# Latent attention: transposing the probabilities in groups of eight instead of four, and what moves with them

## The chip, the cores and the metric

One NeuronCore of a Trainium2 chip runs the kernel. The metric is the device time of one execution in microseconds. Three runs of the kernel before took 1213.33, 1215.23 and 1217.88 us; their median is 1215.23. A lower time is better. The engines are named as in the profile: PE is the tensor engine (PEld its weight loads), DVE the vector engine, ACT the scalar engine, POOL GpSimd, SP the engine that issues most transfers.

## The reference

The kernel computes one layer of an encoder on 1024 tokens of width 1024, in float32. A normed input goes through one wide projection. Its parts feed two mixers. Mixer A is a latent attention with 8 heads, dense over all 1024 tokens; mixer B is an attention with dilated windows in three groups of 8 heads. Each mixer's output is multiplied by a gate, projected, gated again, and the two are added, projected once more, added to the input, and normed. The part that the change touches is mixer A:

```python
def one_block(q_blk):
    s = jnp.einsum('bqhd,bkhd->bhqk', q_blk, k).astype(jnp.float32)
    p = jax.nn.softmax(s, axis=-1).astype(v.dtype)
    return jnp.einsum('bhqk,bkhd->bqhd', p, v)
```

Queries and keys have 96 numbers a head, values 64.

## The kernel before

**Precision.** A float32 operand is split in a high and a low part, each in the format fp32r that PE multiplies in one go. `mm3` (lines 143 to 147) makes a product of two split operands in three matmuls: high by high, high by low, low by high. In the trace these are L145, L146 and L147.

**Stages.** The input projection, the dilated mixer, the latent attention (797.4 to 1087.5 us of the span) and the output projection follow one another. All of it is issued in the order in which it is written (`manual_schedule`): each engine has one queue and takes its instructions in that order. An instruction that waits holds up all that stands behind it on its engine.

**The latent attention** works through 32 units. A unit is one head and 256 of the queries, that is two blocks of 128 queries, called b = 0 and b = 1. Units come in pairs: an even unit and the odd unit behind it fill the two halves of one PSUM bank with their weighted values. `mla_attention` (from line 1187) calls `mla_tick(k, c)` four times for each unit k, with c = 0 to 3. A tick issues work of three units at once:

- *Transposes.* The probabilities of unit k lie with queries on the partitions, and the value product needs the keys there. `mla_transposes` (L1063) turns one group: four tiles of 128 by 128, two key blocks by two query blocks, into one PSUM bank. The banks for this are a ring of two, `pt`. Four groups c = 0 to 3 make a unit.
- *High and low part.* ACT copies the bank to `pt_h` (L1065), DVE subtracts that from the bank into `pt_l` (L1071, `mla_low`). `pt_h` and `pt_l` are rings of two as well, so a group's copy reuses the buffer of the group before the last, which its value product must have read.
- *Value product.* `mla_values(k, c)` makes four matmuls of 256 columns (L1087 with the high part, L1088 with the low part) and adds them up in the bank `m_av`. Group 0 of an even unit starts that bank anew.
- *Scores of the next unit.* `mla_scores(k + 1, b)` makes six matmuls of 512 columns (L145 to L147 into `left` or `right`), `mla_maxima` takes the row maxima on DVE (L1047), `mla_exponentials` the exponentials on ACT (L1055, with a read-out of their sum).
- *After an odd unit*, `mla_copied` copies one half of the partitions of `m_av` on ACT (L1094) and `mla_sum` adds it to the other on DVE (L1103). These run in tick 0 of the next, even unit.
- *After the last unit of a pair of heads and a half of the queries* (units 5, 7, 13, 15, 21, 23, 27, 31), `mla_spread` transposes the denominators on PE (L1117) into the next bank of the same ring `pt`, and DVE doubles and inverts them (L1119, L1120). Then follow transfers, a product on POOL (`mla_gated`), one on DVE (`mla_weighted`, L1140) and a split on ACT and POOL (`mla_merged`).
- *Feed.* In ticks 2 and 3, `feed` issues some steps of other projections, so that PE has work while ACT and DVE turn the groups over; a step is one `mm3` of 512 columns. Up to unit 7 these belong to the gates of the input projection, behind it to the projections of the mixers' outputs. The number of steps to a tick is `rate`: 2 in most units, 1 in units 11, 12, 16, 17, 21, 22, 26 and 27.

The order of one unit on PE was, with T for four transposes, S for six score matmuls, V for four value matmuls and F for a feed:

```
tick 0: T(k,0)  S(k+1,0)  V(k-1,3)  [denominators]
tick 1: T(k,1)  S(k+1,1)  V(k,0)
tick 2: T(k,2)  F         V(k,1)
tick 3: T(k,3)  F         V(k,2)
```

After a tick, `mla_attention` runs what has fallen due of the dilated mixer's last sums (DVE L1636, POOL L1640) and of the loads of the last weights.

Of the kernel before, what the change touches and what calls it, by code (L numbers as in the profile page):

```python
# [11 lines left out]
F32R = mybir.dt.float32r  # L12
# [49 lines left out]
class Net:  # L62
# [994 lines left out]
    def mla_transposes(self, k, c):  # L1057

        pt = self.get("pt")
        for c2 in range(2):  # L1060
            for b in range(2):
                kc, o = 2 * c + c2, c2 * 256 + b * 128
                self.nc.tensor.transpose(pt[:, o:o + 128], self.P[k, b][:, 128 * kc:128 * kc + 128], self.ident)  # L1063
        h, l = self.get("pt_h", dtype=F32R), self.get("pt_l", dtype=F32R)
        self.nc.scalar.copy(out=h, in_=pt)  # L1065
        self.pt[k, c] = pt, h, l

# [82 lines left out]

    def mla_tick(self, k, c):

        self.mla_transposes(k, c)
        if c == 0:
            self.mla_low(k, c)
            self.mla_scores(k + 1, 0)
            self.mla_values(k - 1, 3)
            self.mla_copied(k - 1)
            self.mla_spread(k)
            self.mla_maxima(k + 1, 0)  # L1160
            self.mla_sum(k - 1)
            h, u = self.units[k - 1] if k else (0, 0)
            if u == 3 and h < 6:
                self.mla_load_v(h + 2)
        elif c == 1:
            self.mla_exponentials(k + 1, 0)
            self.mla_low(k, c)
            self.mla_scores(k + 1, 1)
            self.mla_values(k, 0)
            self.mla_maxima(k + 1, 1)  # L1170
            self.mla_weighted(k - 1)
            h, u = self.units[k]
            if u == 3 and h < 6:
                self.mla_load_qk(h + 2)
        else:
            if c == 2:
                self.mla_exponentials(k + 1, 1)
            self.mla_low(k, c)
            self.feed(self.rate)
            self.mla_values(k, c - 1)  # L1180
            if c == 2:
                for n in {6: (), 7: (), 8: (5,), 9: (7,)}.get(k, (k - 1,)):
                    self.mla_merged(n, self.nc.gpsimd)
            else:
                self.mla_gated(k)
# [714 lines left out]
```

## Time and profile before

| | us |
|---|---|
| median of three runs | 1215.23 |
| lowest and highest run | 1213.33, 1217.88 |
| the profiled execution | 1215.87 |
| its span (first to last instruction) | 1214.1 |
| PE busy | 1197.5 |
| DVE busy | 739.8 |
| ACT busy | 606.1 |
| POOL busy | 557.5 |

A row of the profile's groups names line, engine, operation, tiles and shapes, then the count, the total busy time in us, the mean of one in ns, and the idle time of the engine just before, with what ended it. A row of the timeline begins with the start and the length of an instruction in us from the span's start; rows that end in x4 are four instructions in one, and a bracket gives idle time of the engine and what ended it. The ends of matmuls are modelled, so the distance from one start to the next tells what a matmul costs, not its length. A row of the stretches gives bounds and length in us, the busy time (and count) of PE, PEld, DVE, ACT and POOL, the granted clock of PE as a share of full speed, and the load of the DMA engines. The tiles of the latent attention show as `bank` (the rings `pt`, `m_av` and `pj`), `left` and `right` (scores), `at_r` and `at_f` (placed by hand in SBUF) and `m_nm` (maxima).

### The profile page before, as it was taken

To read this page: it belongs to the slowest core of one execution; us is meant where nothing else is said; L and a number is where in the kernel's file an instruction comes from. 1 tells how busy PE (TensorE), PEld (TensorE's weight loads), DVE (VectorE), ACT (ScalarE), POOL (GpSimd) and SP (SyncE) were. 2 spreads that over 40 slices of the span, in tenths; PEclk is the share of its full clock that TensorE was granted. 3 is DMA by queue.
4 is the path that set the end of the run, shared out by engine and by line. 5 is a ranking of instruction groups with operands and counts; after the bars stand their busy time and mean duration, and the time that the engine had idled before them with its cause. 6 is when DMAs were issued, how large, how long until landed. Compare 5 with 4: busy or idle time off the path is not lost.

```text
span 1214.1 us, 18210 instructions
## 1 busy us (share of the span) xinstructions
PE 1197.5 (99%) x6343; PEld 1030.1 (85%) x6343; DVE 739.8 (61%) x1289; ACT 606.1 (50%) x1259; POOL 557.5 (46%) x473
## 2 busy tenths in 40 slices
PE   9999999999999999999999999999999999999997
PEld 8888878888888888889889899888888888888886
DVE  6775447466666653345666666566757767669442
ACT  6633346343434435356565657454655656654222
POOL 1413027877777777544374624335820111258322
PEclk9999999999999999999999999999999999999999
DMA  8757983597355642397899898937462534235141
GB/s 282 227 192 267 330 311 108 195 281 194 106 139 153 177 122 108 101 289 212 239 258 274 247 263 245 260 107 188 137 171 78 139 105 123 79 121 181 74 154 52
DMA packets 128924, 221.30 MB, mean 182 GB/s; under 512 B 28024, under 2 KB 66496, under 8 KB 123904
## 3 DMA queue, kind: packets, MB, share of 16 engines
q1 hardware_dynamic: 128832, 220.14, 60.5%
q8 instruction: 50, 0.82, 0.3%
q14 instruction: 42, 0.34, 0.1%
HBM read 149.24 MB, written 70.85 MB: 181 GB/s over the span
## 4 chain that ended last, share of the span: by engine, by line
PE 89%; DMA 5%; POOL 2%; DVE 1%; ACT 1%; issue 1%; SPq 0%; POOLq 0%; ACTq 0%; DVEq 0%
PE bank L145 7%; PE bank L146 7%; PE bank L147 7%; PE pj L146 5%; PE pj L147 5%; PE pj L145 5%; PE bank L1063 4%; PE st_d L146 2%; PE st_a L146 2%; PE st_c L146 2%; PE st_c L147 2%; PE st_a L147 2%; PE st_d L147 2%; PE st_d L145 2%; PE st_a L145 2%; PE st_c L145 2%
## 5 line engine op out<-in xcount | busy, mean ns | idle before, releaser
L152 POOL TENSOR_TENSOR w_l<-w_raw,w_h 128x512 fp32r<-128x512 f32 x175 | 230.1, 1327 | 213.2 <-ACT w_h L151 164.5
L151 ACT CAST w_h<-w_raw 128x512 fp32r<-128x512 f32 x188 | 111.7, 620 | 121.7 <-POOL w_raw L684 98.1
L145 PE MATMUL bank<-at_r,w_h 128*128 128x512 f32 x344 | 141.6, 412 | 0.0
L146 PE MATMUL bank<-at_r,w_h 128*128 128x512 f32 x344 | 135.4, 394 | 0.5 <-POOL at_r L152 0.5
L147 PE MATMUL bank<-at_r,w_l 128*128 128x512 f32 x344 | 135.5, 394 | 0.0
L1071 DVE TENSOR_TENSOR at_r<-bank,at_r 128x512 fp32r<-128x512 f32 x128 | 87.9, 687 | 69.0 <-ACT at_r L1065 68.5
L1065 ACT CAST at_r<-bank 128x512 fp32r<-128x512 f32 x128 | 74.9, 585 | 85.4 <-PE bank L1063 84.8
L684 POOL TENSOR_TENSOR w_raw<-w_raw 128x512 f32<-128x512 f32 x64 | 83.2, 1300 | 6.3 <-DVE w_l L152 5.6
L1063 PE MATMUL bank<-consts,at_f 128*128 128x128 f32 x512 | 76.9, 272 | 0.5 <-DVE at_r L1071 0.5
L147 PEld LDWEIGHTS bank<-at_r,w_l 128*128 128x128 f32 x344 | 64.8, 188 | 14.5
L146 PE MATMUL pj<-w_l,at_r 128*128 128x512 f32 x192 | 75.5, 393 | 1.2 <-DVE w_l L152 1.2
L145 PE MATMUL pj<-w_h,at_r 128*128 128x512 f32 x192 | 75.7, 394 | 0.7 <-ACT w_h L151 0.7
L1336 DVE TENSOR_TENSOR at_r<-bank,at_r 128x512 fp32r<-128x512 f32 x64 | 43.9, 685 | 53.0 <-ACT at_r L1332 52.7
L147 PE MATMUL pj<-w_h,at_r 128*128 128x512 f32 x192 | 75.4, 392 | 0.0
L146 PEld LDWEIGHTS bank<-at_r,w_h 128*128 128x128 f32 x344 | 65.2, 189 | 9.7 <-POOL at_r L152 1.0
L145 PEld LDWEIGHTS bank<-at_r,w_h 128*128 128x128 f32 x344 | 65.0, 189 | 8.9
L1088 PE MATMUL bank<-at_r,at_r 128*128 128x256 f32 x256 | 67.2, 284 | 4.2 <-DVE at_r L1071 4.2
L1087 PE MATMUL bank<-at_r,at_r 128*128 128x256 f32 x256 | 67.2, 283 | 0.0
L1317 ACT ACTIVATE at_f<-at_f,at_f 128x256 f32<-128x256 f32 x128 | 64.1, 505 | 1.4 <-DVE at_f L1310 1.4
L1332 ACT CAST at_r<-bank 128x512 fp32r<-128x512 f32 x64 | 37.5, 586 | 54.3 <-PE bank L1324 53.1
L1063 PEld LDWEIGHTS bank<-consts,at_f 128*128 128x128 f32 x512 | 59.3, 140 | 1.3 <-DVE at_r L1071 0.9
L1088 PEld LDWEIGHTS bank<-at_r,at_r 128*128 128x128 f32 x256 | 48.7, 190 | 10.2 <-DVE at_r L1071 5.1
(335 smaller groups left out, 3287.1 us busy)
## 6 DMA issues: line engine op xcount, KB each, us to landing
w_raw<-wt SPq DMA_DIRECT2D x48, 512.0 KB, 4.0
at_r<-s_dq SPq DMA_DIRECT2D x32, 512.0 KB, 8.0
s_dk<-dq_st SPq DMA_DIRECT2D x80, 128.0 KB, 2.3
s_dv<-dv_st SPq DMA_DIRECT2D x16, 512.0 KB, 3.4
s_dq<-dq_st SPq DMA_DIRECT2D x64, 128.0 KB, 2.4
zt<-s_gt SPq DMA_DIRECT2D x32, 256.0 KB, 3.8
w_raw<-wv SPq DMA_DIRECT2D x24, 256.0 KB, 5.7
at_r<-s_dk SPq DMA_DIRECT2D x8, 576.0 KB, 11.8
```

Source lines behind the costliest of these rows:

```text
L145: mm(out, lh, rh, start=start, stop=False, skip_group_check=skip)
L146: mm(out, lh, rl, start=False, stop=False, skip_group_check=skip)
L147: return mm(out, ll, rh, start=False, stop=stop, skip_group_check=skip)
L151: self.nc.scalar.copy(out=h, in_=raw)
L152: sub.tensor_tensor(out=l, in0=raw, in1=h.bitcast(F32), op=ALU.subtract)
L684: self.nc.gpsimd.tensor_tensor(out=b[out], in0=b[x], in1=b[y], op=ALU.subtract)
L1063: self.nc.tensor.transpose(pt[:, o:o + 128], self.P[k, b][:, 128 * kc:128 * kc + 128], self.ident)
L1065: self.nc.scalar.copy(out=h, in_=pt)
L1071: self.nc.vector.tensor_tensor(out=l, in0=pt, in1=h.bitcast(F32), op=ALU.subtract)
L1087: mm(out, vv[:, kc], ph[:, x], start=kc == 0, stop=False)
L1088: mm(out, vv[:, kc], pl[:, x], start=False, stop=kc == 7)
L1317: nc.scalar.activation(out=p, in_=p, func=AF.Exp, scale=-1.0, bias=nm, accum_out=den)
```

## The change

Ticks 0 and 2 now issue two groups of transposes each, and ticks 1 and 3 none. The value product of the group in front stands directly behind the eight transposes: in tick 0 that of the unit before, ahead of the scores; in tick 2 that of group 1, ahead of the feed. The copy of the high part is a function of its own. That of the first group of each eight is issued behind the transposes, that of the second behind the value product, whose buffer it reuses. In tick 0 `mla_copied` moves with the value product; in tick 2 the exponential of the second block stands behind the copy of group 3. The maxima, the sum and everything else on DVE keep their order among themselves.

```diff
@@ mla_transposes
-        h, l = self.get("pt_h", dtype=F32R), self.get("pt_l", dtype=F32R)
+        self.pt[k, c] = pt
+
+    def mla_high(self, k, c):
+
+        pt, h, l = self.pt[k, c], self.get("pt_h", dtype=F32R), self.get("pt_l", dtype=F32R)
         self.nc.scalar.copy(out=h, in_=pt)
         self.pt[k, c] = pt, h, l
@@ mla_tick
-        self.mla_transposes(k, c)
+        if c % 2 == 0:
+            self.mla_transposes(k, c)
+            self.mla_transposes(k, c + 1)
+            self.mla_high(k, c)
         if c == 0:
             self.mla_low(k, c)
+            self.mla_values(k - 1, 3)
+            self.mla_high(k, 1)
+            self.mla_copied(k - 1)
             self.mla_scores(k + 1, 0)
-            self.mla_values(k - 1, 3)
-            self.mla_copied(k - 1)
             self.mla_spread(k)
             self.mla_maxima(k + 1, 0)
             self.mla_sum(k - 1)
...
         else:
+            self.mla_low(k, c)
             if c == 2:
+                self.mla_values(k, 1)
+                self.mla_high(k, 3)
                 self.mla_exponentials(k + 1, 1)
-            self.mla_low(k, c)
             self.feed(self.rate)
-            self.mla_values(k, c - 1)
+            if c == 3:
+                self.mla_values(k, 2)
```

The order on PE is then:

```
tick 0: T(k,0) T(k,1)  V(k-1,3)  S(k+1,0)  [denominators]
tick 1: S(k+1,1)  V(k,0)
tick 2: T(k,2) T(k,3)  V(k,1)  F
tick 3: F  V(k,2)
```

## The prediction

> **What bounds the kernel now.** I read the page first (span, busy shares, chain of waits), then what PE waited for, then single units of the latent attention in order of time.
>
> ```profile
> span 1214.1 us, 18210 instructions
> PE 1197.5 (99%) x6343; PEld 1030.1 (85%) x6343; DVE 739.8 (61%) x1289; ACT 606.1 (50%) x1259; POOL 557.5 (46%) x473
> ...
> PE 89%; DMA 5%; POOL 2%; DVE 1%; ACT 1%; issue 1%; SPq 0%; POOLq 0%; ACTq 0%; DVEq 0%
> ```
>
> PE sets the time: busy 99% of the span and 89% of the chain that ended last. So only two things can move it: PE doing fewer or shorter instructions, or PE standing still more or less. The waits of PE from 797.4 to 1087.5 us, which is the whole latent attention, are these three groups (us in total, times, longest), with two stretches of it that show a unit without any stall:
>
> ```profile
> PE bank L1088 <- DVE at_r L1071: 4.2, 3, 2.1
> PE bank L146 <- POOL at_r L152: 0.5, 1, 0.5
> PE bank L1063 <- DVE at_r L1071: 0.5, 1, 0.5
> ```
>
> ```profile
> 929.57:938.79 9.22, 9.22 (x58) 8.11 (x57) 6.98 (x10) 5.68 (x10) 2.59 (x2) 1.00 0.26 95
> 938.79:948.10 9.31, 9.31 (x60) 8.26 (x58) 5.83 (x8) 5.46 (x10) 0.82 (x1) 1.00 0.28 62
> ```
>
> About 5 us of waiting in 290 us: PE has almost nothing to win back here, and a new order must keep every operand as early as the old one did. These two stretches are units 14 and 15. Their decisive rows, unit 14 first:
>
> ```profile
> 929.57 0.60 PE L1063 MATMUL bank<-consts,at_f 128*128 128x128 f32 x4
> 929.92 0.47 PE L145 MATMUL right<-at_r 96*128 96x512 f32 x1
> ...
> 930.20 0.58 ACT L1065 CAST at_r<-bank 128x512 fp32r<-128x512 f32 x1 [1.56 <-PE bank L1063]
> ...
> 931.15 0.40 PE L147 MATMUL right<-at_r 96*128 96x512 f32 x1
> ...
> 931.58 1.23 DVE L1047 TENSOR_REDUCE m_nm<-right 128x1 f32<-128x1024 f32 x1
> ...
> 932.23 0.48 PE L145 MATMUL left<-at_r 96*128 96x512 f32 x1
> 932.54 0.40 PE L146 MATMUL left<-at_r 96*128 96x512 f32 x1
> ...
> 932.78 0.40 PE L147 MATMUL left<-at_r 96*128 96x512 f32 x1
> 932.84 0.68 DVE L1103 TENSOR_TENSOR at_f<-bank,at_f 64x512 f32<-64x512 f32 x1
> ...
> 933.71 0.29 PE L1087 MATMUL bank<-at_r,at_r 128*128 128x256 f32 x1
> ...
> 934.19 0.60 PE L1063 MATMUL bank<-consts,at_f 128*128 128x128 f32 x4
> ```
>
> The reader is to see two chains side by side. On PE: first score block, value product (third group of the unit in front), four transposes, second score block, and at 933.71 value product 0. On DVE: the maxima of the first block (L1047), then the sum of the two value halves (L1103), done at 932.84 + 0.68 = 933.52. Product 0 of an even unit starts a new accumulation in the one PSUM bank that this sum still reads, so it must come after it. Here it comes 0.19 us after. That the cover is thin is seen in who waited for the sum:
>
> ```profile
>   PEld bank L1087: 0.9, 4
> ```
>
> Four weight loads did wait for it, hidden behind the matmul in flight.
>
> **PE's own work.** No instruction is added or removed; order is all that changes. A group of four transposes takes 929.92 − 929.57 = 0.35 us to the next start, and the first 512-column product behind it 932.54 − 932.23 = 0.31 instead of 932.78 − 932.54 = 0.24 (0.23 in most), so 0.08 more: 0.43 in all. Four steps of (0.60 − 0.27)/3 = 0.11 (the mean of one is the 272 ns of the page's group) make 0.44. Entering and leaving transposes thus costs nothing that I can separate from zero. Of 128 groups 64 are joined to the one in front; I take 0.007 us for each, −0.4 us together. Bounds: 0, and −5 us if the whole 0.08 were saved each time.
>
> ```profile
> L1063 PE MATMUL bank<-consts,at_f 128*128 128x128 f32 x512 | 76.9, 272 | 0.5 <-DVE at_r L1071 0.5
> ```
>
> **Even units: the sum is late.** Call s the start of the last matmul of the first score block (931.15 here). The maxima start at s + 0.43. Now the value product and the four transposes that stood behind the first score block move ahead of it, so the second block follows at s + 0.23 and takes 933.71 − 932.23 − 0.08 = 1.40 us: product 0 is ready at s + 1.62. The sum, still behind the maxima on DVE, starts 932.84 − 931.58 = 1.26 after them here, and 1.14 in unit 18:
>
> ```profile
> 965.80 1.23 DVE L1047 TENSOR_REDUCE m_nm<-right 128x1 f32<-128x1024 f32 x1
> ...
> 966.94 0.67 DVE L1103 TENSOR_TENSOR at_f<-bank,at_f 64x512 f32<-64x512 f32 x1
> ```
>
> It ends at s + 0.43 + 1.14 + 0.67 = 2.25 to s + 2.37, PE follows 0.05 later. PE stands 0.68 to 0.80 us, in each of the 15 units 2, 4, ... 30: I take 0.75, **+11.2 us**. Behind the wait are the transposes of groups 2 and 3, then everything else on PE.
>
> **Units that spread a denominator (5, 7, 13, 15, 21, 23, 27).** Here a transpose of the denominators (L1117) takes a turn of the two-bank ring, and two small DVE operations precede the maxima:
>
> ```profile
> 940.38 0.40 PE L147 MATMUL right<-at_r 96*128 96x512 f32 x1
> ...
> 941.10 0.27 PE L1117 MATMUL bank<-consts,m_den 128*8 128x128 f32 x1
> ...
> 941.40 0.28 DVE L1119 TENSOR_SCALAR at_f<-bank 8x128 f32<-8x128 f32 x1 [0.67 <-PE bank L1117]
> ...
> 941.72 0.94 DVE L1120 RECIPROCAL at_f<-at_f 8x128 f32<-8x128 f32 x1
> ...
> 942.59 1.15 DVE L1047 TENSOR_REDUCE m_nm<-right 128x1 f32<-128x1024 f32 x1
> ...
> 943.67 0.66 DVE L1071 TENSOR_TENSOR at_r<-bank,at_r 128x512 fp32r<-128x512 f32 x1
> ```
>
> L1117 to the end of the low part of group 1 (L1071) is 943.67 + 0.66 − 941.10 = 3.23 us. After the change L1117 stands right behind the score block; PE needs from it 0.03 + 0.08 + 1.40 + 0.48 (product 0: 934.19 − 933.71) = 1.99 us until the transposes of group 2. Their ring turn is now the bank of group 1, which that low part still reads: they wait 3.23 + 0.05 − 1.99 = 1.29 us. Seven units: **+9.0 us**. Before, a feed and the transposes of group 2 lay between, into the other bank.
>
> **Plain odd units.** The low part of group 1 follows the maxima: s + 0.43 + 1.14 + 0.69 + 0.05 = 2.31, and the transposes of group 3 want its bank at s + 1.62 + 0.48 + 0.44 = 2.54. Slack 0.23, cost 0. One other DVE operation ahead of it (0.69) would take 0.46 in each of 8 units: upper bound +3.7.
>
> **High parts and the second exponential.** The exponential of the second block now stands on ACT behind the high part of group 3, which needs product 1 (it reuses its buffer). Its rows in unit 11:
>
> ```profile
> 910.39 1.12 ACT L1055 ACTIVATE at_f<-left,m_nm 128x1024 f32<-128x1024 f32 x1
> ...
> 911.40 0.20 ACT L1055 ACTIVATION_READ_ACCUMULATOR at_f<-left,m_nm 128x1 f32 x1
> ```
>
> That is 1.21 us with its read-out. From the start q of the transposes of group 3: product 1 begins at q + 0.35, its third matmul at about q + 0.68, ACT follows 0.3 later (930.20 against a fourth transpose at 929.90), 0.58 for the copy, 1.21 for the exponential: the probabilities are there at about q + 2.8 to 2.9. PE asks for them with the second transpose of the next unit: 0.35 + 0.08 + 0.48 for group 3 and product 1, two slots of feed at 0.70 a step (half of the 1.40), 0.48 for product 2 and 0.11. With one step a slot (units 11, 12, 16, 17, 21, 22, 26, 27) that is q + 2.9, with two steps q + 4.3. In those eight units the cover is nearly gone: I take +0.3 in all, bounds 0 and 8 × 0.35 = +2.8.
>
> **Where PE already stood still.**
>
> ```profile
> 845.57 0.69 DVE L1636 TENSOR_TENSOR at_f<-at_f,at_f 128x512 f32<-128x512 f32 x1 [5.07 <-DMA at_f<-s_rr]
> ...
> 846.92 0.39 PE L1088 MATMUL bank<-at_r,at_r 128*128 128x256 f32 x1 [1.88 <-DVE at_r L1071]
> ...
> 887.42 0.69 DVE L1003 SCALAR_TENSOR_TENSOR at_f<-zt,bank 128x512 f32<-128x512 f32 x1 [5.28 <-DMA zt<-s_gt]
> ...
> 888.76 0.38 PE L1088 MATMUL bank<-at_r,at_r 128*128 128x256 f32 x1 [2.11 <-DVE at_r L1071]
> ...
> 1059.88 0.50 PE L146 MATMUL bank<-at_r,w_h 128*128 128x512 f32 x1 [0.55 <-POOL at_r L152]
> ```
>
> Two late transfers hold DVE, and PE behind it. PE reaches the first later (1.5 us of new stalls lie ahead of it) and the load of values that goes ahead of that transfer on SP's queue is freed earlier, as its product moves ahead of the scores: −1. At the second the low part of group 1 is late too, +0.3. At 1059.88 the cast that POOL waits for stands behind the later exponential: +0.9. Unit 31, with a denominator and no scores, +0.7. Together +0.9; bounds −6 (all of them vanish) and +4.
>
> **Sum.** −0.4 + 11.2 + 9.0 + 0.3 + 0.9 = +21 us. The profiled execution took 1215.87 us, span 1214.1 and 1.8 around it; the median of the runs, 1215.23, is 0.6 less. 1215.9 + 21 − 0.6 gives **1236 us**. The bounds: low −5 + 15 × 0.68 + 9 − 6 = +8 with everything at its end, +13 with the switches at −0.4; high 15 × 0.80 + 9 + 3.7 + 2.8 + 4 = +31. The forecast's own range is 1228 to 1246.
>
> **Rivals.** *One of the two waits is not paid* (DVE gets to the sum, or to the low part, in time): 1225 to 1227. For it: neither wait stands in the old trace, both starts are worked out. Against: both follow from the order on one engine and from rows that agree to 0.1 us. 9%.
>
> *The clock falls.* The second late transfer was followed by a stretch at half clock:
>
> ```profile
> 889.57 0.62 PE L145 MATMUL bank<-at_r,w_h 128*128 128x512 f32 x1
> ...
> 892.13 0.41 PE L1087 MATMUL bank<-at_r,at_r 128*128 128x256 f32 x1
> ...
> 892.98 0.70 PE L1063 MATMUL bank<-consts,at_f 128*128 128x128 f32 x4
> ...
> 893.43 0.48 PE L145 MATMUL bank<-at_r,w_h 128*128 128x512 f32 x1
> ```
>
> That is 3.86 us for what takes 1.48 + 0.48 + 0.35 = 2.31 elsewhere: 1.55 lost. If the seven new waits of 1.29 us, each followed by 0.87 us of transposes, did this, +11: 1247. Against it: after the similar wait that ended at 846.92 the clock held. 6%. The Trainium skill (TensorE: Matmul & The Clock Gate, Part 4: PE-mode transpose) says that transposes don't count as busy for the clock, which would join wait and transposes to one idle stretch. The trace doesn't bear it out so far: granted clock 1.00 in both units above.
>
> *The other side: leaving and entering transposes costs more than four rows show*, and joining groups saves it. It decides from 21 / 64 = 0.33 us a join on; with the bound of 0.08 (−5) and the two waits unpaid it gives 1210, with the measured 0.007 and the waits unpaid 1215, no change. Against: the sum of 0.43 against 0.44. 11%, of which 4% faster. That the order doesn't change at all is excluded: PE follows the written order row by row.
>
> **Chances.** Forecast 74%, one wait 9%, clock 6%, other side 11%. Faster by over 0.5% (6 us, what a measurement of this kernel can tell) 4%, within 7%, slower 89%. The range from 1225 to 1247 holds the forecast, most of the first rival and half of the second.
>
> **What would show it.** In the changed profile: PE waiting at L1087 for DVE's sum in even units, 0.7 us each, and at the transposes for L1071 in the seven spreading units, 1.3 us each; count and length of PE's instructions as before; clock 1.00. Wrong if the waits of PE in this phase stay near 5 us, or if transposes in eights run at another pace than 0.11 us each.

## The result, and the profile after

The changed kernel takes 1237.15 us (median of 5 runs, 1233.5 to 1238.62) against 1215.23 us: a ratio of 1.0171, 95% interval 1.0153 to 1.019. It is slower by 1.7%. The profiled execution took 1237.15 us with a span of 1235.4.

The page of the changed kernel, its span, busy times and chain by engine:

```profile
span 1235.4 us, 18217 instructions
...
PE 1201.1 (97%) x6343; PEld 1029.8 (83%) x6343; DVE 739.4 (60%) x1289; ACT 608.8 (49%) x1259; POOL 556.6 (45%) x473
...
PE 84%; DMA 6%; DVE 5%; issue 2%; POOL 1%; ACT 1%; SPq 1%; POOLq 0%; ACTq 0%; DVEq 0%
```

The same 6343 matmuls, and the other engines busy for about as long as before. PE is idle for 34.3 us of the span against 16.6, and busy 3.6 us more with the same work. DVE, 1% of the chain before, now holds 5%. The waits of PE (us in total, times, longest):

```profile
PE bank L1063 <- DVE at_r L1075: 11.5, 9, 2.6
PE bank L1091 <- DVE at_f L1107: 9.1, 15, 0.7
...
PE bank L146 <- POOL at_r L152: 0.9, 1, 0.9
```

Lines have moved: L1071 is now L1075 (low part), L1103 is L1107 (sum), L1087 is L1091, L1117 is L1121 and L1636 is L1647. Fifteen waits of the value product for the sum, and nine of the transposes for a low part. Units 14 and 15 as stretches (bounds, length, busy times of PE, PEld, DVE, ACT, POOL, granted clock, DMA):

```profile
936.87:946.93 10.06, 9.39 (x59) 8.07 (x58) 6.90 (x10) 5.75 (x10) 1.21 (x2) 1.00 0.17 56
946.93:957.59 10.66, 9.51 (x59) 8.19 (x58) 6.78 (x10) 5.68 (x10) 1.29 (x2) 1.00 0.31 81
```

They are 0.84 and 1.35 us longer than before, at full clock. The rows of the changed kernel that show why, in order of time; unit 14, then unit 15:

```profile
936.87 1.04 PE L1063 MATMUL bank<-consts,at_f 128*128 128x128 f32 x8
...
939.38 0.39 PE L147 MATMUL right<-at_r 96*128 96x512 f32 x1
...
939.81 1.23 DVE L1047 TENSOR_REDUCE m_nm<-right 128x1 f32<-128x1024 f32 x1 [0.99 <-PE right L147]
...
941.06 0.68 DVE L1107 TENSOR_TENSOR at_f<-bank,at_f 64x512 f32<-64x512 f32 x1
...
941.80 0.39 PE L1091 MATMUL bank<-at_r,at_r 128*128 128x256 f32 x1 [0.67 <-DVE at_f L1107]
...
949.68 0.27 PE L1121 MATMUL bank<-consts,m_den 128*8 128x128 f32 x1
...
949.99 0.28 DVE L1123 TENSOR_SCALAR at_f<-bank 8x128 f32<-8x128 f32 x1 [1.11 <-PE bank L1121]
...
950.30 0.94 DVE L1124 RECIPROCAL at_f<-at_f 8x128 f32<-8x128 f32 x1
...
951.17 1.15 DVE L1047 TENSOR_REDUCE m_nm<-right 128x1 f32<-128x1024 f32 x1
...
952.25 0.66 DVE L1075 TENSOR_TENSOR at_r<-bank,at_r 128x512 fp32r<-128x512 f32 x1
...
952.97 1.09 PE L1063 MATMUL bank<-consts,at_f 128*128 128x128 f32 x8 [1.15 <-DVE at_r L1075]
```

In unit 14 the sum ends 2.36 us after the start of the last score matmul (941.74 − 939.38) and product 0 follows 0.06 later. The DVE chain has kept its length to 0.01 us (2.37 before); PE has come to its end sooner. In unit 15 it is 3.23 us from L1121 to the end of the low part (952.91 − 949.68), exactly the length before, and the eight transposes of groups 2 and 3 wait for its end.

Two other places moved, in opposite directions. Unit 5, where a late transfer holds DVE:

```profile
845.52 0.60 PE L1063 MATMUL bank<-consts,at_f 128*128 128x128 f32 x4
...
847.42 0.69 DVE L1647 TENSOR_TENSOR at_f<-at_f,at_f 128x512 f32<-128x512 f32 x1 [4.42 <-DMA at_f<-s_rr]
...
848.77 0.66 PE L1063 MATMUL bank<-consts,at_f 128*128 128x128 f32 x4 [2.65 <-DVE at_r L1075]
...
850.68 0.63 PE L145 MATMUL right<-at_r 96*128 96x512 f32 x1
```

and the stretch behind that wait:

```profile
849.74:854.19 4.45, 4.45 (x16) 3.30 (x15) 1.74 (x3) 0.58 (x1) 4.29 (x4) 0.62 0.69 208
```

The second group of transposes waits 2.65 us there (1.88 us before, at a product), and a score matmul behind it takes 0.63 us instead of 0.39: the granted clock of the stretch is 0.62. In unit 9, which had the other long wait and the half clock before, neither is there now.

### The profile page after: what moved, and what is told of

The parts are those of the page before. It is cut to its first block, busy times and chain, and to the rows that moved or that the text cites. A ratio compares the mean times of both kernels' runs of the same rounds, so it can differ in the third digit from the quotient of the medians.

```text
span 1235.4 us, 18217 instructions
## 1 busy us (share of the span) xinstructions
PE 1201.1 (97%) x6343; PEld 1029.8 (83%) x6343; DVE 739.4 (60%) x1289; ACT 608.8 (49%) x1259; POOL 556.6 (45%) x473
## 4 chain that ended last, share of the span: by engine, by line
PE 84%; DMA 6%; DVE 5%; issue 2%; POOL 1%; ACT 1%; SPq 1%; POOLq 0%; ACTq 0%; DVEq 0%
PE bank L145 6%; PE bank L146 6%; PE bank L147 6%; PE pj L146 5%; PE pj L147 5%; PE pj L145 5%; PE bank L1063 4%; PE bank L1091 2%; PE st_a L145 2%; PE st_a L146 2%; PE st_a L147 2%; PE st_d L145 2%; PE st_c L145 2%; PE st_c L146 2%; PE st_d L146 2%; PE st_d L147 2%
## 5 line engine op out<-in xcount | busy, mean ns | idle before, releaser
L145 PE MATMUL bank<-at_r,w_h 128*128 128x512 f32 x344 | 136.0, 395 | 0.2 <-ACT at_r L151 0.2
L146 PE MATMUL bank<-at_r,w_h 128*128 128x512 f32 x344 | 134.5, 391 | 0.9 <-POOL at_r L152 0.9
L1075 DVE TENSOR_TENSOR at_r<-bank,at_r 128x512 fp32r<-128x512 f32 x128 | 87.0, 685 | 39.8 <-ACT at_r L1069 38.5
L1069 ACT CAST at_r<-bank 128x512 fp32r<-128x512 f32 x128 | 74.8, 586 | 69.0 <-PE bank L1063 53.0
L1091 PE MATMUL bank<-at_r,at_r 128*128 128x256 f32 x256 | 73.2, 308 | 9.1 <-DVE at_f L1107 9.1
L1063 PE MATMUL bank<-consts,at_f 128*128 128x128 f32 x512 | 67.2, 273 | 11.6 <-DVE at_r L1075 11.5
L1055 ACT ACTIVATE at_f<-right,m_nm 128x1024 f32<-128x1024 f32 x32 | 35.7, 1116 | 67.5 <-DVE m_nm L1047 67.5
L1092 PE MATMUL bank<-at_r,at_r 128*128 128x256 f32 x256 | 66.5, 282 | 0.0
```

The source lines that it names most:

```text
L145: mm(out, lh, rh, start=start, stop=False, skip_group_check=skip)
L146: mm(out, lh, rl, start=False, stop=False, skip_group_check=skip)
L1075: self.nc.vector.tensor_tensor(out=l, in0=pt, in1=h.bitcast(F32), op=ALU.subtract)
L1091: mm(out, vv[:, kc], ph[:, x], start=kc == 0, stop=False)
L1092: mm(out, vv[:, kc], pl[:, x], start=False, stop=kc == 7)
```

## The experiments

All edits are small changes of order. This table sums them up; a unit is measured from the start of its first transposes to that of the next unit's, the attention from the first transposes to the start of the last value matmul, both in the profiled execution. There is one such execution of each kernel, so these columns are single measurements. The ratios below are to runs of the kernel before that were made alongside (medians 1215.38 and 1216.05 us), not to the 1215.23 us of the table. Unit 14 stands for the even units, 15 for those that spread denominators, 19 for the plain odd ones.

| kernel | median us | unit 14 | 15 | 19 | 5 | 9 | attention |
|---|---|---|---|---|---|---|---|
| before | 1215.23 | 9.23 | 9.31 | 9.20 | 11.53 | 13.17 | 289.99 |
| changed | 1237.15 | 10.06 | 10.67 | 9.13 | 14.48 | 9.13 | 310.20 |
| sum first | 1230.48 | 9.46 | 10.64 | 9.13 | 15.54 | 10.26 | 305.66 |
| spread late | 1226.97 | 10.09 | 9.45 | 9.13 | 11.12 | 10.49 | 299.95 |
| both | 1222.27 | 9.44 | 9.42 | 9.13 | 11.38 | 13.33 | 294.90 |
| product back | 1230.05 | 9.61 | 10.66 | 9.15 | 15.26 | 10.08 | 304.97 |
| product ahead (fours) | 1223.12 | 9.67 | 9.32 | 9.20 | 14.28 | 10.31 | 298.99 |
| early load | 1232.80 | 10.06 | 10.66 | 9.13 | 10.93 | 9.91 | 309.05 |
| all | 1217.20 | 9.13 | 9.43 | 9.13 | 10.20 | 13.55 | 289.98 |
| early load (fours) | 1213.58 | 9.21 | 9.31 | 9.20 | 9.31 | 13.17 | 287.74 |

**Sum first.** On the changed kernel, one swap on DVE in tick 0:

```diff
-            self.mla_maxima(k + 1, 0)
             self.mla_sum(k - 1)
+            self.mla_maxima(k + 1, 0)
```

> The changed kernel with one swap on DVE: in tick 0 the sum of the value halves goes ahead of the maxima of the first score block. Theory (the sum is late because it stands behind the maxima): the sum can start when the copy on ACT is done, and ends about 0.8 us behind the start s of the last score matmul instead of 2.3, while product 0 of the even unit is ready at s + 1.62. The waits of PE at L1091 for the sum (9.1 us seen, 11.4 by starts) vanish; the maxima are 0.3 us later, which leaves the transposes of group 3 at about 0.05 us of wait. Time 1237 - 11 = 1226 us (1224 to 1229). Rival (PE waits there for something else that is late too, the low part of group 1 or the second exponential): the wait moves to the transposes, and the time falls by less than 4 us, to 1233 or more.

Measured: 1230.48 us, ratio to before 1.012 (1.0105 to 1.0136); 6.7 us less than the changed kernel, between theory and rival. Its waits:

```profile
PE bank L1063 <- DVE at_r L1075: 14.0, 12, 3.1
```

The waits for the sum are gone altogether, and unit 14 is 0.60 us shorter: the place of the sum was the cause. Three things were missed. A wait of 0.2 us is left at the transposes of even units where I expected 0.05 (below, "both"). Units 5 and 9, where transfers are late, lost 1.1 us each without any edit there. And unit 31 lost 1.6 us to a stretch at half clock in this execution (last section).

**Spread late.** On the changed kernel, the denominators' work behind the low part of group 1:

```diff
@@ tick 0
-            self.mla_spread(k)
@@ tick 1
             self.mla_low(k, c)
+            self.mla_spread(k)
             self.mla_scores(k + 1, 1)
```

> The changed kernel, with the denominators' work called in tick 1 behind the low part of group 1 instead of in tick 0 ahead of the maxima. PE keeps its order; on DVE the two small operations follow the low part. Theory (the low part is late by the two operations, and holds the bank of the group-2 transposes): the wait of 1.31 us in units 13, 15, 21, 23, 27, 7 and 0.73 in unit 5 shrinks to about 0.1, some of unit 31's 1.6 goes too; 1237 - 8.5 = 1228.5 us (1226 to 1231). Rival (the second maxima and the second exponential, now 1.2 us later, hold the next unit's transposes instead): the time falls by less than 4 us.

Measured: 1226.97 us, ratio 1.0093 (1.0078 to 1.0108). Its waits:

```profile
PE bank L1091 <- DVE at_f L1107: 9.0, 15, 0.7
PE bank L1063 <- DVE at_r L1075: 2.1, 2, 1.5
```

The sum's 15 waits stand as before, 9 of the 11.5 us at the transposes are gone; unit 15 went from 10.67 to 9.45. The theory holds, the rival falls. Unit 5 had a shorter wait and kept its clock in this execution (11.12 us against 14.48, where a spreading unit's saving is 1.2), unit 31 fell by 1.4, and unit 9 grew by 1.4. Together these would account for the 1.5 us by which the time is below what was expected. Unit 5 was shorter because its transfer came sooner: DVE went on 10.9 us after the start of unit 4, where it was 12.1 in the changed kernel and 12.7 in "sum first". None of the three kernels edits the issue of that transfer; what moves its landing stays open.

**Both.**

> Both edits of the two runs above together. Theory: the two waits are separate and their savings add, 1237 - 11 - 8.5 = 1217.5 us (1214 to 1221), so that the order with eights comes out near the old one. Rival: eights have a cost of their own beside the two waits (clock, copies held by the ring of two): 1224 us or more.

Measured: 1222.27 us, ratio 1.0057 (1.004 to 1.0075), runs from 1219.18 to 1225.73. The two savings add in the units (9.44 and 9.42), but 1222 is nearer to the rival's 1224 than to 1217.5, so the trace had to say what was left. Unit 14 of this kernel, ACT and DVE:

```profile
932.26 0.59 ACT L1069 CAST at_r<-bank 128x512 fp32r<-128x512 f32 x1 [0.21 <-PE bank L1091]
...
932.88 0.58 ACT L1098 COPY at_f<-bank 64x512 f32<-64x512 f32 x1
...
933.49 0.68 DVE L1107 TENSOR_TENSOR at_f<-bank,at_f 64x512 f32<-64x512 f32 x1 [0.71 <-ACT at_f L1098]
...
934.21 1.23 DVE L1047 TENSOR_REDUCE m_nm<-right 128x1 f32<-128x1024 f32 x1
...
935.35 0.68 DVE L1075 TENSOR_TENSOR at_r<-bank,at_r 128x512 fp32r<-128x512 f32 x1
```

The sum waits 0.71 us for the copy of its half (L1098), which stands on ACT behind the high part of group 1 (L1069). So the maxima start 0.43 us later than the scores allow (934.21 against 933.78), the low part ends at 936.03, and the transposes of group 3 wait for it. That makes 0.31 us in unit 14 against a plain unit, some 4 us in 15 units: the next operation in line, which "all" below moves. Unit 9 had its long wait and half clock again in this execution (13.33 us against 9.13).

**Product back.** On the changed kernel, the value product of the unit in front behind the scores again:

```diff
-            self.mla_values(k - 1, 3)
-            self.mla_high(k, 1)
-            self.mla_copied(k - 1)
             self.mla_scores(k + 1, 0)
+            self.mla_values(k - 1, 3)
+            self.mla_copied(k - 1)
+            self.mla_high(k, 1)
```

> The changed kernel with transposes in eights, but the value product of the unit in front (with its copy on ACT, and behind that the copy of the high part of group 1) put back behind the first score block. Theory (what was lost is PE work between the first score block and product 0): four value matmuls, 0.48 us, stand there again, so the wait in the 15 even units falls from 0.8 (wait and slow first matmul) to about 0.3, -7 us; the wait of the spreading units stays at 1.3, as the denominators' transpose moves with the product: 1230 us (1227 to 1232). Rival (the eights cost, not the place of the product): 1235 to 1239.

Measured: 1230.05 us, ratio 1.0113 (1.01 to 1.0127), as the theory had it. Unit 14 fell by 0.45 us, near the 0.48 of the four matmuls that are cover again, and unit 15 stayed at 10.66.

**Product ahead, in fours.** The kernel before with that one part of the change:

```diff
-            self.mla_scores(k + 1, 0)
             self.mla_values(k - 1, 3)
             self.mla_copied(k - 1)
+            self.mla_scores(k + 1, 0)
```

> The kernel before, transposes in fours, with one part of the change alone: in tick 0 the value product of the unit in front and its copy on ACT go ahead of the first score block. Theory: product 0 of an even unit is then ready 0.48 us earlier, at s + 2.05 against the sum at s + 2.30 to 2.42, a wait of 0.25 to 0.37 in 15 units, +4.5 us: 1219.7 us (1217 to 1222). The spreading units don't wait, since the four transposes of group 1 still stand between the denominators and group 2. Rival (the product's place is free, the grouping in eights costs): 1215 us, no change.

Measured: 1223.12 us, ratio 1.0065 (1.0051 to 1.0079): slower, against the rival, but by 7.7 us and not 4.5. Its waits:

```profile
PE bank L1088 <- DVE at_r L1071: 5.4, 7, 3.1
...
PE bank L1087 <- DVE at_f L1103: 1.4, 7, 0.2
```

Even units grew by 0.44 (unit 14), near the 0.37 worked out; the first matmul behind a wait makes up 0.1. What I had not worked out is the first row: the product that comes 1.5 us sooner needs the low part of its own group sooner, and waits for it seven times, most of all in unit 5, where that low part stands behind the late transfer. No eights are needed to lose time here; cover in front of a DVE result is what counts.

**Early load.** On the changed kernel, the transfer behind which unit 5 waits, issued at step 9 of the dilated mixer's last sums and not at step 10, two ticks earlier:

```diff
         def step9():
             for half in range(2):
                 weighted(0, half, v)
                 add(1, half)
+            spread(2, 0, halves[1])
             self.turn["bc"] = 1
         def step10():
-            spread(2, 0, halves[1])
             weighted(2, 0, v)
```

> The changed kernel, with the transfer that unit 5 waits for (the last spread of the dilated mixer's shares) issued two ticks earlier; only its place in SP's order changes. Theory (PE waits in unit 5 for a low part that stands behind this transfer on DVE, and the half-clock stretch behind it follows from that wait): the wait of 2.65 us at the transposes of unit 5 and the 1.7 us of slow clock behind it go, 1237 - 4.4 = 1232.7 us (1231 to 1235). Rival (the transfer lands when the loads in front of it on the DMA engines are done, not when it is issued): it lands less than 1.5 us earlier and the time stays at 1235 to 1238.

Measured: 1232.8 us, ratio 1.0142 (1.0124 to 1.016), as the theory had it. Unit 5 fell from 14.48 to 10.93 us, and its half-clock stretch is gone. The rival was half right all the same: in this kernel DVE still waits for the transfer's data,

```profile
845.71 0.69 DVE L1647 TENSOR_TENSOR at_f<-at_f,at_f 128x512 f32<-128x512 f32 x1 [1.82 <-DMA at_f<-s_rr]
```

and goes on 9.5 us after the start of unit 4 (836.21) against 12.1 in the changed kernel (835.32). The transfer is two DMAs on SP; against the start of unit 4 they are issued 3.7 and 4.4 us sooner, and DVE goes on 2.6 us sooner. That was enough.

**All.** Sum first, spread late, early load, and on ACT the copy of the value half ahead of the high part of group 1:

```diff
             self.mla_values(k - 1, 3)
-            self.mla_high(k, 1)
             self.mla_copied(k - 1)
+            self.mla_high(k, 1)
```

> The changed kernel with the sum ahead of the maxima, the denominators behind the low part of group 1, the earlier transfer, and on ACT the copy of the value half ahead of the copy of the high part of group 1. Theory: with the sum and denominators moved the time was 1222.3; the 0.19 to 0.29 us that even units still lost there come from the sum waiting for that copy, -3.7, and the earlier transfer gives -2.3: 1216.3 us (1213 to 1219), level with the old order. Rival (eights have a cost of their own): 1220 or more.

Measured: 1217.2 us, ratio 1.0003 (0.9989 to 1.0018). Unit 14 is now 9.13 us, and its sum starts with the copy's end:

```profile
931.07 0.58 ACT L1098 COPY at_f<-bank 64x512 f32<-64x512 f32 x1 [0.34 <-PE bank L1092]
...
931.68 0.68 DVE L1107 TENSOR_TENSOR at_f<-bank,at_f 64x512 f32<-64x512 f32 x1 [0.23 <-ACT at_f L1098]
```

The latent attention of this kernel, of the kernel before, and of the kernel before with the same earlier transfer (next run), as stretches:

```profile
797.59:1087.60 290.01, 284.73 (x1741) 251.31 (x1740) 200.18 (x260) 171.64 (x302) 94.24 (x81) 0.99 0.45 122
```

```profile
797.40:1087.40 290.00, 284.79 (x1741) 251.34 (x1740) 201.82 (x260) 169.75 (x302) 94.23 (x81) 0.99 0.44 122
```

```profile
797.79:1085.50 287.71, 284.36 (x1740) 251.38 (x1739) 202.44 (x260) 169.79 (x302) 93.96 (x81) 0.99 0.45 124
```

"All" is level with the kernel before only because it has the earlier transfer and that kernel doesn't. The fair partner is the third row: against it the eights still cost 2.3 us in the attention, and 3.6 us in the medians (1217.20 against 1213.58). They win 0.06 to 0.10 us in most plain units, but units 4, 5 and 28 are longer by 1.1, 0.9 and 0.55, and the other spreading units up to unit 27 by 0.11 to 0.19. Unit 4 shows how:

```profile
832.48 1.56 DVE L1647 TENSOR_TENSOR at_f<-at_f 128x512 f32<-128x512 f32 x2 [1.37 <-DMA at_f<-s_rr]
833.96 0.68 DVE L1075 TENSOR_TENSOR at_r<-bank,at_r 128x512 fp32r<-128x512 f32 x1
...
834.70 0.66 PE L1063 MATMUL bank<-consts,at_f 128*128 128x128 f32 x4 [0.46 <-DVE at_r L1075]
```

The low part of the group in front stands on DVE behind work that waited for a transfer, and the second group of transposes wants its bank at once; in fours the first score block lay between. So these edits bring the eights near the old order but not level with it; most of what is left sits where DVE or POOL is late for another reason.

**Early load, in fours.** The kernel before with the earlier transfer alone:

> The kernel before, with the same transfer issued two ticks earlier. Theory: the 1.9 us for which PE waits in unit 5 go, nothing else: 1215.3 - 2 = 1213.3 us (1212 to 1215). Rival (the transfer lands as late as before): 1215.3.

Measured: 1213.58 us, ratio 0.9978 (0.9967 to 0.9989). Unit 5 falls from 11.53 to 9.31, nothing else moves. It is the fastest version found, 0.2% below the kernel before, and has no part of the change in it.

## Why the prediction was right

The time (1236 against 1237.15) and its two main terms were right. That it came within 1.2 us is partly luck, since smaller errors cancelled. In the profiled executions the span grew by 21.3 us, of which 20.2 in the attention, 1.1 ahead of it, where the code is the same, and nothing behind it (126.7 us in both). The 21.3 are +12.6 in the even units (11.2 forecast), about +9.5 in the spreading ones (9.0), −0.5 in the other units without a wait (−0.4 and +0.3 were forecast for PE's own work and the second exponential), −1.4 in what is left of units 5, 9 and 31 (+0.9, which counted unit 28 in), and the 1.1 ahead (none).

*Even units, +11.2.* The mechanism is the one given: the waits for the sum are there 15 times, 0.67 us in unit 14, and "sum first" takes them away. The lateness was right too: by the starts, product 0 of unit 14 comes 1.06 us behind the score matmul in front (941.80 − 940.74) where 0.23 is the pace, so it is 0.83 late, and 0.80 was the upper figure worked out. (The bracket shows 0.67 because the modelled end of that score matmul lies 0.16 behind the pace.) The sum was short by the price of starting again, which it had left out: the first matmul behind the wait takes 0.22 us to the next start instead of 0.12. Unit 14 grew by 0.84, the 15 units (4 and 28 with them) by 12.6 us.

*Spreading units, +9.0.* Right: a wait of 1.29 was worked out for each, and unit 15 grew by 1.35; six of them (without unit 5) grew by 8.1 us, and "spread late" takes 1.22 of it away.

*Plain odd units and the second exponential, 0 and +0.3.* Right: units 1, 3, 11, 17, 19, 25 and 29 don't wait. They are 0.04 to 0.07 us shorter.

*PE's own work, −0.4.* Inside its bounds, but too small: with the −0.07 us of unit 19 in each unit it is about −2 us. The starts in unit 19 show where it comes from. Entering and leaving transposes, and the slower first matmul behind them, change by 0.006 us together, near the 0.014 that 0.007 for each of two joins would make. The other 0.06 are 24 products of 512 columns that follow each other a little faster in the new order (last section).

*Where PE already stood still, +0.9.* The step that failed. Unit 5 was to win 1 us beside its wait as a spreading unit, and lost 1.6 (2.95 in all less 1.35); unit 9 was to lose 0.3 and won 4.0. For unit 5 I moved the landing of the transfer with its place in SP's queue. It was issued 0.4 to 1.0 us sooner against unit 4, as forecast, but DVE went on 12.1 us after the start of unit 4, 11.8 before. Meanwhile the wait itself moved forward: the transposes of group 1 now need, 1.5 us sooner, the same low part for which the product of the unit in front waited before. The wait became 0.8 us longer, and the half clock behind it, about 1.7 us, had not been counted for this unit at all. For unit 9 I left out that the gate's load was issued sooner against the unit (3.7 us after the start of unit 8, 4.4 before) and that unit 8 had become 0.8 longer; and the load itself landed 7.9 us behind its issue where it was 10.0 before, which is the largest part and whose cause stays open. It landed 1.5 us after the start of unit 9 and not 5.1. Both units are single executions: in the other kernels with eights unit 9 lies between 9.9 and 13.6 us. Unit 28 grew by 1.38 (an even unit's 0.75 and the wait for POOL) and unit 31 with the last product by 1.1, near what was given.

*The rivals.* The clock did not fall for the new waits: unit 15 waits 1.15 us, transposes for 0.87, and has a granted clock of 1.00. By the Trainium skill (TensorE: Matmul & The Clock Gate, Part 4: PE-mode transpose) transposes don't count as busy for the clock in the same way, so both together would make one idle stretch of 2.0 us. The trace doesn't bear that out: the clock stayed in all six units with this wait, though the margin is thin against the waits of 1.96 us and up that were followed by a lower clock (last section). It did fall once, behind the 2.65 us of unit 5. "One wait not paid" is excluded by the two rows of waits. "Switches cost more" is excluded by the plain units: two joins go with 0.07 us less, 0.035 each, where this rival needed 0.33.

## What to carry to other kernels

Where PE is busy 99% of the time, its order still matters, since instructions of PE are the cover under which other engines get ready: before moving one forward, find the result that the instruction behind the gap needs, and count the microseconds from the same starting event on both engines. A result's lateness is set by what stands ahead of it on its own engine, here a row maximum and two operations on 8 partitions, and reordering those alone won back 15 of the 22 us here ("both"). A wait that hangs on a transfer doesn't follow from the order on the engines alone: between these kernels it came and went in unit 9 without an edit to it. If the transfer can be issued early, as here, do that first. And compare two orders with the same extras on both sides: "all" looked level with the kernel before, and is 0.3% behind it once both have the earlier transfer.

## What the runs showed that was not expected

Waits of PE in the attention from 1.96 us up were each followed by one stretch at half clock: 1.96 ("both"), 2.1 (before, unit 9, and early load in fours), 2.6 ("all", unit 9), 2.65 (changed), 2.9 to 3.1 (sum first, product back, product ahead). After 1.88 (before, unit 5), 1.73 ("both", unit 5) and 1.5 us ("spread late") the clock stayed. A stretch costs 1.55 us on top of the wait by the prediction's rows. From the 0.62 over 4.45 us it lasts (1 − 0.62) / 0.5 × 4.45 = 3.4 us, and half of that is 1.7. The length of a single wait does not settle it, however. In two executions ("sum first", "early load") such a stretch came in unit 31 behind waits of only 0.5 and 1.4 us close together, while the same two waits in the changed kernel and in "product back" had none behind them. What decides there stays open; both executions were the slowest of their kernel's runs.

In unit 19 of the changed kernel, where no run of 512-column products begins behind transposes, most went at 0.227 us a matmul; those right behind value products began at about 0.235 for the first one. In the same unit before, the runs behind four transposes went at 0.231 after a first one of 0.315. The cause of the 0.004 is open.
